# An order for every engine from one list scheduler at build time, in a streaming-encoder block on one core

## The chip, the core and the metric

The kernel runs on one core of a Trainium2 chip, as one launch. The metric is device time in microseconds (us); what is shown is the median of three runs. Below, PE is TensorE's matmul pipe and PEld its weight load, DVE is VectorE, ACT is ScalarE, POOL is GpSimd, SP is SyncE, whose queue issues nearly all DMAs. L319 is line 319 of the program named.

## The reference

256 tokens of width 2048 (`x`) and 256 memory tokens (`mem`) pass through one layer, all in float32; D_FF is 5632.

```python
x = x + 0.5 * swiglu(rms_norm(x, ffn1_norm), ffn1_w_gate, ffn1_w_up, ffn1_w_down)
h = rms_norm(x, mix_norm);  proj = h @ w_in
u, q, k, v, g, a_lr = split(proj)       # 1024 | 512 | 512 | 1024 | 1024 | 16 columns
y_pool = pool_mixer(u, pool_w, pool_scale)              # trailing means over 2/4/8/16 tokens
y_gla  = gla_mixer(q, k, v, g, a_lr, w_a2, b_a, head_norm)   # chunks of 64, 4 heads
x = x + concat([y_pool, y_gla]) @ w_out
x = x + mem_cross_attention(rms_norm(x, xattn_norm), rms_norm(mem, mem_norm), w_q, w_kv, w_o)
x = x + 0.5 * swiglu(rms_norm(x, ffn2_norm), ffn2_w_gate, ffn2_w_up, ffn2_w_down)
out = rms_norm(x, final_norm)
# swiglu(h, g, u, d) = (silu(h @ g) * (h @ u)) @ d
```

## The kernel before, in words

**Units.** All weights are streamed once, in units of 1 MB: a `raw` tile of 128 x 2048 floats. For precision, each unit is split in two: ACT casts `raw` to `wh` (the high part, in the chip's reduced float32 form), DVE subtracts `wh` from `raw` to give `wl` (the low part). Activations are split likewise (`xs` and `ys`, each with a high and a low half). PE then forms three products (high by high, high by low, low by high) and adds them in PSUM; a usual unit is 24 matmuls of 128 x 512. So every unit is a chain: a DMA on SP's queue, a cast on ACT, a subtraction on DVE, 24 matmuls on PE. There are three buffers each of `raw`, `wh` and `wl`. In these names the first number is the unit's: `wh24` is the high part of unit 24.

**Blocks.** Units are gathered in blocks which accumulate in PSUM. PSUM holds four tiles `ps` of two banks; each block takes two of them (`pt`), or four, or one, and gives them back when its results are evicted. `block_t` is the usual one. `block_s`, used for the gate and up projections of the two FFNs, takes three of its eight units (`PAIRS`, 0, 2 and 4) as seven products of sums in the place of eight: DVE makes sums `T` of weights (`add_weights`), and such a unit has a second pair of casts (`xh`, `xl`). It holds all four PSUM tiles; after its last unit, `combine` and `join` fold the four with additions on DVE into a tile `sg` in SBUF. A block behind it needs the PSUM tiles that these read.

**What stands between blocks.** `st.op(f, n)` hangs a piece of other work n units further on: the turning of the hidden layer's result (`turn`: 8 transposes `ph` on PE, a cast and a subtraction into `ys`), the next norm (`fold`: 8 transposes `px`, 8 scaled casts into `xs` on ACT and 8 on DVE, two squares for the norm on ACT), the mixer's and the attention's vector work. Program order is that of `Stream.emit`: splits run two units ahead of the matmuls.

**Who sets the order.** In the two FFN sections (`ordered(True)` to `ordered(False)`) DVE and ACT keep program order; there ACT and DVE run what `Stream.emit` wrote, whatever waits. Elsewhere, and on PE everywhere, the framework's own scheduler may reorder. At the start `x_squares` is held behind the scaled cast of its chunk by `tc.issue_after`. At the end `ready_sqrt` puts an activation with a square root on ACT, in program order, so that the function table is loaded before the last norm needs it.

**Places the prediction speaks of.** Unit 24 (the first unit of a `block_s` that stands behind another `block_s`, whose last two accumulators `pt44` and `pt45` its joins add into `sg46`); the fold around unit 129 between FFN1 and the mixer; the pool part's `k` additions around unit 151; the first four units; the last norm.

Of the kernel before, what the change touches and what calls it, by code (L numbers as in the profile page):

```python
# [1 line left out]

# [90 lines left out]
class Ordered:  # L93


    def __init__(self, tc, engine):
        self.tc, self.engine = tc, engine

    def __getattr__(self, name):
        f = getattr(self.engine, name)  # L100

        def call(*args, **kw):
            return self.tc.keep_in_program_order(f(*args, **kw))  # L103

        return call


class Engines:


    def __init__(self, tc):
        self.nc, self.ordered = tc.nc, False
        self.pinned = {n: Ordered(tc, getattr(tc.nc, n)) for n in ("vector", "scalar")}

    def __getattr__(self, name):
        if name in ("vector", "scalar") and self.ordered:
            return self.pinned[name]
        return getattr(self.nc, name)


def build(ctx, tc, I, out):
    nc = Engines(tc)
# [8 lines left out]
    scope = {"stack": None}  # L131

    def open_scope(name):
        def f():
            scope["stack"] = ExitStack()
            scope["pool"] = scope["stack"].enter_context(
                tc.tile_pool(name=name, bufs=1, reuse_waits="tile")
            )
        return f

    def close_scope():
        scope["stack"].close()
        scope["stack"] = None

    def ptile(name):
        return psum.tile([P, 2, NB], F32, tag="ps", name=name)
# [10 lines left out]
    def ctile():  # L157
        return scope["pool"].tile([P, 2, S], F32, tag="c", name=uid("c"), bufs=2)

    def ttile():  # L160
        return scope["pool"].tile([P, 2, S], F32, tag="t", name=uid("t"), bufs=3)
# [3 lines left out]
    def whole_lines(pool, shape, dt, tag, name, bufs=1):  # L165
# [4 lines left out]
        t = pool.tile([shape[0], -(-n // LINE) * LINE], dt, tag=tag, name=name, bufs=bufs)[:, :n]  # L170
# [10 lines left out]
    ident = head.tile([P, P], F32, tag="ident", name="ident")  # L181
    make_identity(tc.nc, ident)
    ones = const.tile([P, P], F32, tag="ones", name="ones")
# [13 lines left out]
    X = [dram.tile([S, 2 * NB], F32, tag=f"X{b}", name=f"X{b}") for b in range(2)]  # L197
    xs = main.tile([P, KT, 2, S], F32R, tag="xs", name="xs")
    ys = main.tile([P, KT, 2, S], F32R, tag="ys", name="ys")
# [28 lines left out]
    def diagonal(col):  # L228
        d = scope["pool"].tile([P, P], F32, tag="diag", name=uid("diag"), bufs=4)
        nc.vector.tensor_scalar_mul(d, ident, col)  # L230
        return d
# [20 lines left out]
    def row_squares(src, c):  # L252

        for h in range(2):
            j = tmp.tile([P, S], F32, tag="j", name=uid("j"), bufs=2)
            nc.scalar.activation(j, src[h], AF.Square, accum_out=ss[:, h, c : c + 1])
# [10 lines left out]
    def spread_norm():  # L267
# [4 lines left out]
        R = rows["R"] = scope["pool"].tile([P, S], F32, tag="R", name=uid("R"))  # L272
# [80 lines left out]
    def part_sums(act, ext, i, g):  # L353

        t = scope["pool"].tile([P, 4 * NB], F32, tag="T", name=uid("T"))
# [15 lines left out]
    def add_weights(u, raw):  # L371
        t = scope["pool"].tile([P, 4 * NB], F32, tag="T", name=f"T{u}")
# [9 lines left out]
    def split_seven(u, raw, t):  # L382
        th, tl = (
            wpool.tile([P, 4 * NB], F32R, tag=n, name=f"{n}{u}", bufs=st.AHEAD + 1)
# [5 lines left out]
        if True:  # L390
            r = [
                scope["pool"].tile([P, 3 * NB], F32R, tag=n, name=f"{n}{u}", bufs=2)
# [28 lines left out]
    def block_s(srcs, act, ext, pairs, evict, delays=(0, 0)):  # L421
# [32 lines left out]
        def combine():  # L454

            e = held["e"] = scope["pool"].tile([P, 4, NB], F32, tag="sg", name=uid("sg"), bufs=2)
# [89 lines left out]
    def gain_columns(names, queue):  # L546
        t = rows["gain"] = scope["pool"].tile([P, P], F32, tag="gain", name=uid("gain"), bufs=2)
# [11 lines left out]
    def x_tile(b):  # L559
        xrows[b] = scope["pool"].tile([P, 2, 2 * NB], F32, tag="sg", name=uid("x"), bufs=2)  # L560
# [35 lines left out]
    def x_squares(c):  # L596
        with tc.issue_after(rows["hi", c].ins):
            row_squares([x_cols(c * S, S)[:, h] for h in range(2)], c)
# [31 lines left out]
    def fold(c, gain):  # L630
# [10 lines left out]
        for h in range(2):  # L641
            q = tmp.tile([P, NB], F32, tag="j", name=uid("j"), bufs=2)
# [19 lines left out]
    def pair_sums(g, delay):  # L662
        def f():
            if g == PAIRS[0]:
                rows["xe"] = scope["pool"].tile(
# [11 lines left out]
    def ordered(on):  # L677
        def f():
            nc.ordered = on
        return f  # L680

    def ffn(wg, wu, wd, down):
        gate = {}
        st.op(ordered(True), 8)

        def hidden():
            e = scope["pool"].tile([P, 4, NB], F32, tag="sg", name=uid("sg"), bufs=2)
# [67 lines left out]
    st.op(ordered(False))  # L755
# [7 lines left out]
    def mt(name, shape, tag=None, bufs=1):  # L763
        t = whole_lines(scope["pool"], shape, F32, tag or name, uid(name), bufs)
# [14 lines left out]
    def m4():  # L779
        return scope["pool"].tile([P, 2 * 2 * (S + PAD)], F32, tag="m4", name=uid("m4"), bufs=3)  # L780
# [264 lines left out]
    def xt(name, shape, dt=F32, tag=None, bufs=1):  # L1045
        t = whole_lines(scope["pool"], shape, dt, tag or name, uid(name), bufs)
# [118 lines left out]
    def last_gain():  # L1165
        fin["gB"] = scope["pool"].tile([P, D], F32, tag="T", name="gB")
        nc.sync.dma_start(fin["gB"], I["final_norm"].partition_broadcast(P))

    def down_last(wd, k0, nk, last):
        if last:  # L1170
            st.op(ordered(False), 2)
# [4 lines left out]
    def down_end(wd, k0, nk):  # L1176
# [28 lines left out]
        def end_evict(nb, h):  # L1205
            cols = slice(nb * NB, (nb + 1) * NB)
            if h == 0:
                t = scope["pool"].tile([P, 3 * NB], F32, tag=("xh", "xl")[nb % 2], name=uid("O"), bufs=2)
# [38 lines left out]
        def ready_sqrt():  # L1247
            tc.keep_in_program_order(nc.scalar.activation(sums, Rcol, AF.Sqrt))
# [24 lines left out]
    def load(u):  # L1273
        raws[u] = wpool.tile([P, 4 * NB], F32, tag="raw", name=f"raw{u}", bufs=st.RAW)
        st.units[u][0](raws[u])

    def split_unit(u, own):
        raw = raws.pop(u)
        if own is split_seven:
            return split_seven(u, raw, summed.pop(u))  # L1280
        parts = [
            wpool.tile([P, 4 * NB], F32R, tag=t, name=f"{t}{u}", bufs=st.AHEAD + 1)
# [50 lines left out]
```

## Time and profile before

| what | value |
|---|---|
| time, three runs | 2141.07, 2144.1, 2147.86 us; median 2144.1 |
| profiled execution, first to last instruction | 2142.1 us |
| time of the profiled execution outside its span | not recorded; its span is 2.0 below the median of the runs |
| mean granted TensorE clock | 0.997 |
| PE busy | 2117.4 us, 99% of the span |
| DVE busy | 1434.5 us, 67% |
| ACT busy | 1004.6 us, 47% |
| bytes read from HBM | 417.58 MB, 203 GB/s over the span |

The profile is of one execution. A timeline row reads: start in us, length in us, engine, line, operation, result <- operands, sizes, count, and in brackets the idle time ahead of it with what released it. A row of the view of waits reads: engine, what waited, its line, <- what released it: total us, count, the longest. A windows row reads, for a stretch of time: its length, then for each engine its busy us and count, and then the granted PE clock, DMA share and GB/s. Busy time of PE is no measure of how well it is fed; its waits are.

### The profile page before, as it was taken

What the parts mean: (1) busy time and instruction counts of PE and PEld (TensorE: products, weight loads), DVE (VectorE), ACT (ScalarE), POOL (GpSimd) and SP (SyncE); (2) the same over time, 40 slices, a digit from 0 to 9 for tenths busy, and PEclk for the clock granted to TensorE, in tenths of its full rate; (3) what the DMA queues carried; (4) which work ended last, traced back from release to release, by engine and by line L of the source; (5) the groups of instructions that cost most, each with busy time, mean ns of one, the idle gap of its engine ahead of it and who ended that gap; (6) DMA issues with size and microseconds to landing.
All of it is one profiled execution on the core that took longest, in us unless ns stands there. A gap on an engine that the chain in (4) does not pass through costs nothing.

```text
span 2142.1 us, 24059 instructions
## 1 busy us (share of the span) xinstructions
PE 2117.4 (99%) x10032; PEld 1770.8 (83%) x10032; DVE 1434.5 (67%) x1189; ACT 1004.6 (47%) x890; POOL 14.2 (1%) x41
## 2 busy tenths in 40 slices
PE   9999999999999999999999999999999999999998
PEld 7878888888888888888888888888888888888886
DVE  8876588865874676565656545567974788658754
ACT  7544345533543545455445444445453454434533
POOL 0000000000000000000000000000000000000001
PEclk9999999999999999999999999999999999999999
DMA  7556565666566655558655455665666655766673
GB/s 276 177 176 240 212 216 180 209 240 214 197 216 236 218 163 175 177 154 300 228 184 177 157 160 174 197 206 188 198 233 220 212 200 184 252 211 212 216 236 118
DMA packets 143316, 435.91 MB, mean 203 GB/s; under 512 B 9828, under 2 KB 13000, under 8 KB 142824
## 3 DMA queue, kind: packets, MB, share of 16 engines
q1 hardware_dynamic: 143176, 434.38, 60.2%
q8 instruction: 78, 1.28, 0.2%
q14 instruction: 30, 0.25, 0.0%
q10 hardware_dynamic: 32, 0.01, 0.0%
HBM read 417.58 MB, written 16.78 MB: 203 GB/s over the span
## 4 chain that ended last, share of the span: by engine, by line
PE 96%; DVE 2%; ACT 1%; issue 1%; DMA 0%; SPq 0%; DVEq 0%; ACTq 0%
PE pt L319 57%; PE pa L304 15%; PE pt L416 11%; PE pb L319 6%; PE pe L319 3%; PE ph L712 1%; ACT wh L103 1%; PE pl L1106 1%; PE pv L1141 1%; PE px L636 0%; DVE T L103 0%; DVE wl L103 0%; DVE xl L103 0%; DMA x<-in_x 0%; ACT wh L246 0%
## 5 line engine op out<-in xcount | busy, mean ns | idle before, releaser
L319 PE MATMUL pt<-wh,xs 128*128 128x512 f32 x1952 | 618.6, 391 | 0.0
L103 DVE TENSOR_TENSOR wl<-raw,wh 128x2048 fp32r<-128x2048 f32 x186 | 425.1, 2289 | 246.4 <-ACT wh L103 246.4
L319 PE MATMUL pt<-wh,ys 128*128 128x512 f32 x1728 | 535.2, 390 | 0.0
L103 ACT CAST wh<-raw 128x2048 fp32r<-128x2048 f32 x186 | 355.1, 1914 | 378.9 <-PE pt L319 326.5
L247 DVE TENSOR_TENSOR wl<-raw,wh 128x2048 fp32r<-128x2048 f32 (+2 forms) x142 | 314.6, 2216 | 254.5 <-ACT wh L246 254.2
L319 PEld LDWEIGHTS pt<-wh,xs 128*128 128x128 f32 x1952 | 368.0, 189 | 76.3
L246 ACT CAST wh<-raw 128x2048 fp32r<-128x2048 f32 (+2 forms) x143 | 263.1, 1840 | 281.9 <-PE pt L319 96.1
L319 PE MATMUL pt<-wl,xs 128*128 128x512 f32 x976 | 381.3, 391 | 0.0
L319 PEld LDWEIGHTS pt<-wh,ys 128*128 128x128 f32 x1728 | 324.4, 188 | 67.1
L319 PE MATMUL pt<-wl,ys 128*128 128x512 f32 x864 | 336.4, 389 | 1.4 <-DVE wl L103 1.4
L304 PE MATMUL pa<-xs,wh 128*128 128x512 f32 x896 | 317.2, 398 | 2.1 <-DVE t L278 1.7
L304 PE MATMUL pa<-xs,wl 128*128 128x256 f32 x896 | 248.7, 281 | 0.0
L319 PEld LDWEIGHTS pt<-wl,xs 128*128 128x128 f32 x976 | 184.2, 189 | 37.9
L304 PEld LDWEIGHTS pa<-xs,wh 128*128 128x128 f32 x896 | 167.7, 188 | 41.4 <-issue 2.0
L319 PEld LDWEIGHTS pt<-wl,ys 128*128 128x128 f32 x864 | 162.2, 188 | 35.1 <-DVE wl L103 1.9
L103 ACT CAST wh<-T 128x2048 fp32r<-128x2048 f32 x52 | 99.4, 1912 | 151.5 <-PE pt L319 93.2
L304 PEld LDWEIGHTS pa<-xs,wl 128*128 128x128 f32 x896 | 169.1, 189 | 1.6 <-issue 0.2
L103 DVE TENSOR_TENSOR wl<-T,wh 128x2048 fp32r<-128x2048 f32 x52 | 119.0, 2289 | 55.6 <-ACT wh L103 55.2
L319 PE MATMUL pb<-wh,xs 128*128 128x512 f32 x384 | 121.7, 392 | 0.5 <-DVE ys L239 0.5
L416 PE MATMUL pt<-wh,xe 128*128 128x512 f32 x324 | 112.4, 391 | 0.2
L103 DVE TENSOR_TENSOR sg<-pt,sg 128x1024 f32<-128x1024 f32 (+1 forms) x90 | 90.1, 1008 | 6.4 <-ACT sg L103 5.1
L103 DVE TENSOR_TENSOR xl<-raw,xh 128x1536 fp32r<-128x1536 f32 x52 | 91.1, 1751 | 0.0
(213 smaller groups left out, 1820.3 us busy)
## 6 DMA issues: line engine op xcount, KB each, us to landing
raw<-in_ffn_w_down SPq DMA_DIRECT2D x88, 1024.0 KB, 5.4
raw<-in_ffn_w_up SPq DMA_DIRECT2D x80, 1024.0 KB, 5.0
raw<-in_ffn_w_gate SPq DMA_DIRECT2D x77, 1024.0 KB, 5.0
raw<-in_w_in SPq DMA_DIRECT2D x32, 1024.0 KB, 5.2
raw<-in_xattn_w_kv SPq DMA_DIRECT2D x32, 1024.0 KB, 5.2
raw<-in_w_out SPq DMA_DIRECT2D x16, 1024.0 KB, 6.2
raw<-in_xattn_w_q SPq DMA_DIRECT2D x16, 1024.0 KB, 5.2
raw<-in_xattn_w_o SPq DMA_DIRECT2D x16, 1024.0 KB, 5.6
```

The lines of the kernel that those rows point to most:

```text
L103: return self.tc.keep_in_program_order(f(*args, **kw))
L246: nc.scalar.copy(hi, src)
L247: nc.vector.tensor_tensor(out=lo, in0=src, in1=f32(hi), op=ALU.subtract)
L304: nc.tensor.matmul(o, w, x, start=k == 0 and i == 0, stop=last and i == 1)
L319: nc.tensor.matmul(ps, a, w, start=first and i == 0, stop=last and i == 2)
L416: nc.tensor.matmul(banks[n], x, w, start=first and j == 0, stop=not later and n in ("P1", "P5", "P6", "P7") and j == 2,)
L712: nc.tensor.transpose(v[:, i, h * P : (h + 1) * P], g[:, h, i * P : (i + 1) * P], ident)
L1106: nc.tensor.matmul(ps[:, t, :M], ys[:, 4 * h + d, a, tok], xa["K"][:, d, b, :], start=i == 0, stop=i == 11,)
L1141: nc.tensor.matmul(ps[:, d, :S], xa["V"][:, m, a, col], xa["PT"][:, m, b, :], start=i == 0, stop=i == 5,)
```

## The change

Calls such as `nc.vector.tensor_tensor(...)` no longer issue an instruction. A `Recorder` writes each down as a `Task` with the tiles that it reads and writes, and of each tile the cells (64 elements wide, and the rows of partitions) that it touches; two tasks depend on each other if they touch a common cell and one writes. Buffers of a pool are dealt out by `share`: the next user of a place depends on all users of the one before. Each task has a modelled duration (`cost`). `latest` works back from the end along PE's program order to the latest start that holds nothing up; `schedule` then plays the engines forward: PE takes the ready task that is first in program order, the others take, among those ready within `WAIT` (0.2 us), the one with the earliest deadline, with a shorter one ahead if it fits the gap. `emit` issues all in order of the planned starts, and each is kept in that order. `Ordered`, `Engines`, `ordered` and `issue_after` are gone; `ready_sqrt` is recorded as any other task. What is computed, with which instructions on PE, stays as it was.

```diff
-class Ordered:
-    def __init__(self, tc, engine):
-        self.tc, self.engine = tc, engine
+def cost(engine, name, args, kw, writes, reads):
...
+    if name == "dma_start":
+        v = (writes or reads)[0]
+        return dict(busy=0.37, moved=(v.p1 - v.p0) * v.at.size * 4)
+    if engine == "tensor":
+        n = writes[0].at.size
+        busy = 0.2284 if n > 256 else 0.118 if n > 128 else 0.109
+        if name == "matmul" and args[1].dtype is F32:
+            busy = 0.1 + n / 600
+        return dict(busy=busy, tail=0.177)
+    if engine == "scalar":
+        out = writes[0].at.size
+        busy = (0.05 if psum else 0.085) + out * 0.84e-3
...
+        table = {AF.Silu: "silu", AF.Sqrt: "sqrt", AF.Exp: "exp", AF.Ln: "exp"}.get(func)
+        return dict(busy=busy, tail=0.1, table=table)
+    if engine == "vector":
...
+        return dict(busy=(0.13 if name == "scalar_tensor_tensor" else 0.07) + n / 960, tail=0.085)
...
+class Plan:
+    SYNC = 0.034
...
+    def share(self):
+        for bufs, line in self.places.values():
+            held = [None] * bufs
+            for b in sorted((b for b in line if b.users), key=lambda b: b.users[0].i):
+                k = min(range(bufs), key=lambda k: held[k].users[-1].i if held[k] else -1)
+                old, held[k] = held[k], b
+                if old is None:
+                    continue
+                gate = self.add(None, None)
+                for u in old.users:
+                    self.dep(gate, u, False)
+                for u in b.users:
+                    self.dep(u, gate, True)
...
+    def touch(self, t, v, write):
+        b = v.buf
...
+        for c in v.cells():
+            spans = b.cells.setdefault(c, [])
+            keep = []
+            for s in spans:
+                p0, p1, wrote, u = s
+                if p0 < v.p1 and v.p0 < p1:
+                    if write or wrote:
+                        self.dep(t, u, wrote)
+                    if write and v.p0 <= p0 and p1 <= v.p1:
+                        continue
+                keep.append(s)
+            keep.append((v.p0, v.p1, write, t))
+            b.cells[c] = keep
...
+    def ready(self, t, end):
+        r = 0.0
+        for p, data in t.preds.items():
+            if p.engine is None:
+                x = p.start
+            elif p.engine == t.engine and not p.moved and (p.engine == "tensor" or not data):
+                x = p.start + p.busy
+            else:
+                x = end[p.i] + self.SYNC
+            r = max(r, x)
+        return r
+
+    def latest(self):
...
+                left[s.i] -= 1
+                if not left[s.i]:
...
+            late = -t.busy - t.tail
+            for s in t.succs:
+                if t.engine is None:
+                    x = s.late
+                elif t.moved:
+                    x = s.late - 1.8 - t.moved / 338e3
+                elif s.engine == t.engine and (t.engine == "tensor" or not s.preds[t]):
+                    x = s.late - t.busy
+                else:
+                    x = s.late - t.busy - t.tail - self.SYNC
+                late = min(late, x)
+            if t in behind:
+                late = min(late, behind[t].late - t.busy)
+            t.late = late
+
+    def schedule(self):
+        self.share()
+        self.latest()
...
+        def pick(e):
+            q, now = waiting[e], free[e]
+            if e == "tensor":
+                now = max(now, min(t.start for t in q))
+                t = min((t for t in q if t.start <= now), key=lambda t: t.i)
+                return now, t
+            soon = max(now, min(t.start for t in q))
+            u = min((t for t in q if t.start <= soon + self.WAIT), key=lambda t: t.late)
+            if u.start > soon:
+                fit = [t for t in q if t.start <= soon and soon + t.busy <= u.start]
+                if fit:
+                    u = min(fit, key=lambda t: t.late)
+            return max(now, u.start), u
...
+                tables[e] = t.table
+                busy += 1.28
+            free[e] = at + busy
+            end[t.i] = at + busy + t.tail
+            if t.moved:
...
+        self.end = end
+        out = [t for _, _, t in sorted((t.start, k, t) for k, t in enumerate(out))]
+        return out
+
+    WAIT = 0.2
+
+    def emit(self):
+        for t in self.schedule():
+            if t.engine is None:
+                if t.run:
+                    t.run()
+            else:
+                self.tc.keep_in_program_order(t.run())
+
+class Recorder:
...
+            plan, e = self.plan, self.engine
...
+            def run():
+                real = lambda a: a.resolve() if isinstance(a, View) else a
+                f = getattr(getattr(plan.tc.nc, e), name)
+                return f(*(real(a) for a in args), **{k: real(a) for k, a in kw.items()})
+            t = plan.add(e, run, **cost(e, name, args, kw, writes, reads))
...
+            for v in reads:
+                plan.touch(t, v, False)
+            for v in writes:
+                plan.touch(t, v, True)
...
-class Engines:
...
 def build(ctx, tc, I, out):
-    nc = Engines(tc)
+    nc = plan = Plan(tc)
...
     def x_squares(c):
-        with tc.issue_after(rows["hi", c].ins):
-            row_squares([x_cols(c * S, S)[:, h] for h in range(2)], c)
+        row_squares([x_cols(c * S, S)[:, h] for h in range(2)], c)
...
     def ffn(wg, wu, wd, down):
         gate = {}
-        st.op(ordered(True), 8)
...
         def ready_sqrt():
-            tc.keep_in_program_order(nc.scalar.activation(sums, Rcol, AF.Sqrt))
+            nc.scalar.activation(sums, Rcol, AF.Sqrt)
...
     st.emit(load, prepare, split_unit)
+    plan.emit()
```

The order on the engines changes in many places; these are the ones on which the prediction rests. In the changed kernel every operation has the line of the recorder, L469.

**PE around unit 23** (`ph48` and `ph49` are the two transposes of FFN1's first hidden tiles, which read `sg36`; `pt44`, `pt45` the last two accumulators of the block then running). Before, inside unit 23, `ph48` standing in the same way in unit 22:

```order
L319 MATMUL pt44_847<-wh23_1001,xs_107 128x512
L319 MATMUL pt45_848<-wh23_1001,xs_107 128x512
L319 MATMUL pt44_847<-wl23_1002,xs_107 128x512
L712 MATMUL ph49_1045<-ident_73,sg36_560 128x128 x8
L319 MATMUL pt44_847<-wh23_1001,xs_107 128x512 x2
L319 MATMUL pt44_847<-wl23_1002,xs_107 128x512
```

Now:

```order
L469 MATMUL pt45_855<-wh21_930,xs_138 128x512
L469 MATMUL pgain47_1026<-ident_73,gain35_91 128x128
L469 MATMUL ph48_1028<-ident_73,sg36_538 128x128 x8
L469 MATMUL ph49_1041<-ident_73,sg36_538 128x128 x8
L469 MATMUL pt44_847<-wh22_962,xs_138 128x512
L469 MATMUL pt44_847<-wl22_975,xs_138 128x512
```

Both groups of transposes and `pgain47` now stand ahead of unit 22.

**DVE around units 24 to 26** (`T26` is the sum of weights for unit 26; `sg46` takes the results in `pt44` and `pt45` and so gives their PSUM back). Before:

```order
L103 TENSOR_TENSOR ys_108<-ph48_1034,ys_108 128x4x256
L103 TENSOR_TENSOR ys_108<-ph49_1045,ys_108 128x4x256
L103 TENSOR_TENSOR wl24_1057<-T24_997,wh24_1056 128x2048
L103 TENSOR_TENSOR xl24_1061<-raw24_939,xh24_1060 128x1536
L103 TENSOR_TENSOR T26_1090<-raw26_1005 128x1024
L103 TENSOR_TENSOR T26_1090<-T26_1090,raw26_1005 128x512 x2
L103 TENSOR_TENSOR wl25_1095<-raw25_969,wh25_1094 128x2048
L103 TENSOR_TENSOR sg46_992<-pt44_847,sg46_992 128x1024
L103 TENSOR_TENSOR sg46_992<-pt45_848,sg46_992 128x1024
```

Now:

```order
L469 TENSOR_TENSOR xl24_1048<-raw24_955,xh24_985 128x1536
L469 TENSOR_TENSOR ys_1044<-ph48_1028,ys_1044 128x4x256
L469 TENSOR_TENSOR wl24_1071<-T24_1007,wh24_1056 128x2048
L469 TENSOR_TENSOR ys_1044<-ph49_1041,ys_1044 128x4x256
L469 TENSOR_TENSOR T26_1090<-raw26_1030 128x1024
L469 TENSOR_TENSOR T26_1090<-T26_1090,raw26_1030 128x512
L469 TENSOR_TENSOR wl25_1104<-raw25_990,wh25_1092 128x2048
L469 TENSOR_TENSOR sg46_972<-pt44_847,sg46_972 128x1024
L469 TENSOR_TENSOR T26_1090<-T26_1090,raw26_1030 128x512
L469 TENSOR_TENSOR sg46_972<-pt45_855,sg46_972 128x1024
```

`ys48`, the copy of the first transposes, has moved behind `xl24`, and `wl24` between it and `ys49`; the addition from `pt44` stands before the last part of `T26`, and that from `pt45` behind it.

**ACT at the start** (`px` are the transposes of `x`, `j` the squares for the first norm, `chain` the square root; `wh3` the cast of the fourth unit). Before:

```order
L246 CAST wh2_212<-raw2_132 128x1024
L238 ACTIVATE xs_107<-px11_283,gains_97 128x256
L256 ACTIVATE j27_460,ss_100<-x3_125 128x256
L256 ACTIVATE j28_462,ss_100<-x3_125 128x256
L238 ACTIVATE xs_107<-px12_322,gains_97 128x256
L246 CAST xe14_376<-T16_385 128x512
L246 CAST wh3_253<-raw3_167 128x2048
```

Now:

```order
L469 ACTIVATE xs_138<-px10_277,gains_122 128x256 x2
L469 ACTIVATE j31_295,ss_129<-x3_147 128x256
L469 ACTIVATE j32_299,ss_129<-x3_147 128x256
L469 ACTIVATE j33_302,ss_129<-x3_147 128x256
L469 ACTIVATE j34_306,ss_129<-x3_147 128x256
L469 CAST xe14_231<-T16_257 128x512
L469 ACT_TABLE_LOAD
L469 ACTIVATE chain_314<-chain_314 128x2
L469 CAST wh3_332<-raw3_194 128x2048
```

The squares, the load of the square root's table and the square root stand ahead of `wh3`.

**ACT at the fold around unit 129** (`px114`, `px117` the transposes of the new `x`). Before:

```order
L103 CAST wh128_4547<-raw128_4457 128x2048
L103 ACTIVATE xs_107<-px114_4579,gains_97 128x256 x4
L103 ACTIVATE j115_4596,ss_100<-x111_4420 128x512
L103 ACTIVATE j116_4598,ss_100<-x111_4420 128x512
L103 ACTIVATE xs_107<-px117_4600,gains_97 128x256 x4
L103 ACTIVATE j118_4617,ss_100<-x111_4420 128x512
L103 ACTIVATE j119_4619,ss_100<-x111_4420 128x512
L103 CAST wh129_4621<-raw129_4487 128x2048
```

Now:

```order
L469 CAST wh128_4549<-raw128_4479 128x2048
L469 ACTIVATE j115_4561,ss_129<-x111_4128 128x512
L469 ACTIVATE j116_4566,ss_129<-x111_4128 128x512
L469 ACTIVATE j118_4569,ss_129<-x111_4128 128x512
L469 ACTIVATE j119_4572,ss_129<-x111_4128 128x512
L469 CAST wh129_4592<-raw129_4509 128x2048
L469 ACTIVATE xs_138<-px114_4589,gains_122 128x256 x4
L469 ACTIVATE xs_138<-px117_4600,gains_122 128x256 x4
```

The cast of unit 129 has moved ahead of the eight scaled casts into `xs`.

295 lines of the change are left out of this document (243 added, 52 removed).

## The prediction

> **What bounds the kernel now.** I read the page first: the span, the busy times and the chain that ended last.
>
> ```profile
> span 2142.1 us, 24059 instructions
> PE 2117.4 (99%) x10032; PEld 1770.8 (83%) x10032; DVE 1434.5 (67%) x1189; ACT 1004.6 (47%) x890; POOL 14.2 (1%) x41
> PE 96%; DVE 2%; ACT 1%; issue 1%; DMA 0%; SPq 0%; DVEq 0%; ACTq 0%
> ```
>
> PE carries the chain almost from end to end, and the change leaves it the same matmuls. So no more can be won than PE's pauses and the slow stretches that they cause; everything else is under it. The second view is the list of PE's waits:
>
> ```profile
> PE pt L416 <- DVE sg L103: 4.5, 1, 4.5
> PE pgain L554 <- DMA gain<-in_ffn_norm: 4.1, 1, 4.1
> PE pa L304 <- DVE t L278: 1.7, 1, 1.7
> PE pt L319 <- DVE wl L103: 1.4, 1, 1.4
> PE po L976 <- DVE ST L969: 1.0, 1, 1.0
> PE pp L827 <- DVE k L278: 0.6, 1, 0.6
> PE pb L319 <- DVE ys L239: 0.5, 1, 0.5
> PE pa L304 <- DVE xs L239: 0.4, 1, 0.4
> ```
>
> One large wait, six that DVE ends, and the first load (4.1), which no order shortens. Without that load they are 10.1 us. The third view is the windows around the large one, with PE's busy time, its count and, third from the right, its granted clock:
>
> ```profile
> 143.00:148.00 5.00, 0.57 (x3) 0.14 (x1) 4.93 (x6) 0.00 (x0) 0.00 (x0) 0.92 0.65 213
> 148.00:154.00 6.00, 5.93 (x14) 4.67 (x15) 2.66 (x3) 5.89 (x7) 0.00 (x0) 0.50 0.52 173
> 154.00:160.00 6.00, 6.00 (x27) 4.95 (x27) 5.93 (x6) 2.50 (x2) 0.00 (x0) 1.00 0.39 127
> ```
>
> After the pause PE does 14 matmuls in 6 us at clock 0.50, where it does 27 in the next 6 us. At 6.0/27 = 0.222 us each, 14 are worth 3.1, so the slow stretch lost 2.9 us. The pause costs 4.5 + 2.9 = 7.4 us in all. All that is recoverable is then 10.1 + 2.9 = 13.0 us, 0.6% of the span.
>
> **The change part by part.** *The pause at 143 us.*
>
> ```profile
> 128.78 1.03 PE L712 MATMUL ph<-ident,sg 128*128 128x128 f32 x8
> 135.28 1.01 ACT L103 CAST ys<-ph 128x1024 fp32r<-128x1024 f32 x1 [4.42 <-PE ph L712]
> 136.33 1.23 DVE L103 TENSOR_TENSOR ys<-ph,ys 128x1024 fp32r<-128x1024 f32 x1 [4.21 <-ACT ys L103]
> 138.13 2.29 DVE L103 TENSOR_TENSOR wl<-T,wh 128x2048 fp32r<-128x2048 f32 x1 [0.58 <-ACT wh L103]
> 139.89 0.39 PE L416 MATMUL pt<-xh,xs 128*128 128x512 f32 x1
> 140.34 1.75 DVE L103 TENSOR_TENSOR xl<-raw,xh 128x1536 fp32r<-128x1536 f32 x1
> 142.01 1.22 DVE L103 TENSOR_TENSOR T<-raw 128x1024 f32<-128x1024 f32 x1
> 146.80 2.35 DVE L103 TENSOR_TENSOR sg<-pt,sg 128x1024 f32<-128x1024 f32 x2
> 148.07 0.79 PE L416 MATMUL pt<-xh,xs 128*128 128x512 f32 x1 [4.50 <-DVE sg L103]
> ```
>
> The cause is order. ACT and DVE keep program order, and the second transpose's copy (135.28) stands before the cast of unit 24, so both engines idle more than 4 us for a transpose inside unit 23. Then the subtractions `wl24` (2.29), `xl24` (1.75), the sums `T` and `wl25` are all ahead of the two additions that give PSUM back (146.80), and PE waits. In the new order both transposes come before unit 22, at about 127.1 to 129 (16 transposes, twice the 1.03 less overlap), so their casts are done by 132: one cast (1.01), the cast of `wh24`, the second cast. DVE then has, from 129.2 on, `xl24` 1.75, a copy 1.23, `wl24` 2.29, a copy 1.23, a part of `T` 1.22 and about 0.7 for a half of the next, `wl25` about 2.3: 10.7 us, to 139.9. The addition from `pt44` can start when unit 23 ends, at 139.9 + 0.39 = 140.3, and ends at 141.5; the next, behind 0.7 of `T`, at 143.4. PE wants `pt44` at about 143.2, where the old stall began, and `pt45` three matmuls later, 143.9. So the wait goes, with some 0.5 us to spare for the second, and the slow stretch with it: **-7.4**. What is late next would be these additions again, if `T` or `wl25` came 1 us later than I count.
>
> *The fold.*
>
> ```profile
> 704.48 0.47 ACT L103 ACTIVATE xs<-px,gains 128x256 fp32r<-128x256 f32 x1 [4.41 <-PE px L636]
> 713.82 1.90 ACT L103 CAST wh<-raw 128x2048 fp32r<-128x2048 f32 x1
> 718.10 0.50 PE L319 MATMUL pt<-wl,ys 128*128 128x512 f32 x1 [1.44 <-DVE wl L103]
> ```
>
> ACT spends 704.48 to 713.82 on eight scaled casts and four squares before it casts unit 129. The casts now come behind it; at 0.47 each that is at least 3.8 us earlier, more than the wait: **-1.4**. The casts are wanted only by the mixer's first units, behind the rest of FFN1.
>
> *The mixer.*
>
> ```profile
> 832.87 0.69 DVE L278 TENSOR_TENSOR k<-pa,c 128x512 f32<-128x512 f32 x1 [1.41 <-ACT c L277]
> 834.89 2.29 DVE L247 TENSOR_TENSOR wl<-raw,wh 128x2048 fp32r<-128x2048 f32 x1 [0.53 <-ACT wh L246]
> 837.10 0.68 DVE L278 TENSOR_TENSOR k<-pa,c 128x512 f32<-128x512 f32 x1
> ```
>
> A `wl` of 2.29 us stands between two additions of which PE wants the second; now both additions stand before it (wait 0.6, and 0.5 behind it). The others in the list are alike (0.4, 1.0 with its two steps no longer back to back, 1.7 where an accumulator is asked for a unit later). Together 4.2; I leave 0.8 standing, since the 1.7 hangs on an addition behind another long subtraction: **-3.4**. Bounds: 0 to 4.2.
>
> *The start, a loss.*
>
> ```profile
> 11.93 0.47 ACT L238 ACTIVATE xs<-px,gains 128x256 fp32r<-128x256 f32 x1 [0.91 <-PE px L590]
> 22.41 1.91 ACT L246 CAST wh<-raw 128x2048 fp32r<-128x2048 f32 x1
> 24.41 2.28 DVE L247 TENSOR_TENSOR wl<-raw,wh 128x2048 fp32r<-128x2048 f32 x1
> 24.58 0.41 ACT L256 ACTIVATE j<-x 128x256 f32<-128x256 f32 x1
> 26.80 0.60 PE L590 MATMUL px<-ident,x 128*128 128x128 f32 x4
> 42.07 1.28 ACT L217 ACT_TABLE_LOAD   x1
> ```
>
> The cast of unit 3 is at 22.41. Ahead of it ACT now has six more squares (6 x 0.41 = 2.5), three scaled casts fewer (3 x 0.47 = 1.4), and the table load of 1.28 that stood at 42.07, with its square root of 0.2: +2.6. It starts at 25.0 and the subtraction ends 4.3 later (22.41 to 24.41 + 2.28 = 26.69 before), at 29.3. PE now gets to unit 3 at about 26.5, since the four transposes at 26.80 and two like them are placed elsewhere. It can fill 1.1 us with the second half of one chunk's transposes and the first high-by-high products: a pause of about 1.7. Lower bound 0, since ACT idles here now (0.91 in the row at 11.93); upper bound 2.8 without the filling, and with a slow stretch of 2.9 as at 148 it would be 5.7. I take **+1.0**, nearer the low end because ACT's idle time takes part of the work.
>
> The Trainium skill, "TensorE: Matmul & The Clock Gate", Part 1 on the HAM clock gate, says that PE falls to half clock after an idle window of about 3.4 us. By that rule a pause of 2.8 here would leave the clock alone and the upper bound would be 2.8; the one pause of this trace that bears on it (4.5 us, then 0.50) agrees but does not show where the limit lies.
>
> *The hand-overs between blocks.* Nine `block_s` in each FFN end in two joins. The planner takes the ready operation with the earliest deadline, so a `T` or `wl` of the next unit may now stand ahead of a join, or between two.
>
> ```profile
> L103 DVE TENSOR_TENSOR sg<-pt,sg 128x1024 f32<-128x1024 f32 (+1 forms) x90 | 90.1, 1008 | 6.4 <-ACT sg L103 5.1
> ACT xs L238 <- DVE xs L239: 24.3, 21, 2.4
> ```
>
> A join or combine step is an addition of about 1.0 us, and PE wants the next block's accumulators as soon as the last unit ends. The second row shows what the model does not hold: ACT waits for DVE between two reads of one PSUM tile (24.3 us in 21 waits), while the planner, which goes by cells, takes reads of different cells as independent. So planned times can be short. Lower bound 0; upper bound 18 x 0.6 (the wait behind `k` above) = 11. Nearest are the single waits of 0.4 to 0.6, and in most blocks DVE has room: **+1.0**.
>
> The Trainium skill, "PSUM — Partial Sum Buffer", section on bank collisions, asks that two engines not be in one PSUM bank at once, and that software guard it by bank. By that rule the planner's cells are too fine and its order too hopeful; the sum would then go to the upper bound of this term, a rival below.
>
> *The tail.*
>
> ```profile
> 2128.37 0.19 ACT L1214 ACTIVATION_READ_ACCUMULATOR O<-x 128x1 f32 x1
> 2129.82 0.19 ACT L217 ACTIVATE chain<-chain 128x1 f32<-128x1 f32 x1
> ```
>
> The early square root is recorded without a place and is issued so long before that a table load comes back at the end. Between these rows 2129.82 - 2128.56 = 1.26 us are free, and the load takes 1.28: **0**. Without that cover it costs 1.3.
>
> Sum: -7.4 - 1.4 - 3.4 + 1.0 + 1.0 = -10.2 (-12.2 and +2.0). The profiled execution's span becomes 2131.9. It lies 2.0 below the median of the three runs shown (2144.1), so the time is 2144.1 - 10.2 = **2133.9**, called 2134.
>
> **The rivals.** *Most of it is given back* (2138 to 2147). One way: the start takes its 5.7, and the 18 blocks 0.2 each (3.6): 12.2 - 9.3 = 2.9 gained, 2141. The other: the additions from `pt44` stay late and the first term does not come; 4.8 - 2.0 = 2.8, 2141 again. For it: the margin of 0.5 us at 143, and the cells against tiles. Against: both engines idled over 4 us there, which the new order uses.
>
> *Slower than before.* The mechanism is the same collision at other block joins: transposes, casts and `wl` before the additions, in a stretch where DVE has no slack.
>
> ```profile
> 350.00:400.00 50.00, 50.00 (x230) 41.36 (x229) 46.47 (x37) 25.15 (x16) 0.00 (x0) 1.00 0.56 191
> ```
>
> DVE is busy 46.5 of 50 us here, and PE none the less without a pause (50.00): a late addition has 3.5 us in which to catch up. A join that is late as at 143 costs 7.4. Two of them (14.8) eat the 10.2 and leave +4.6, inside what counts as no change; three (22.2) leave +12, 2156. It decides from the second. Against: in the new order an addition stands directly behind the subtraction that it used to follow at a distance.
>
> *More is gained* (2126 to 2129): the losses do not come and the 0.8 that I left in the mixer goes too, all of the 13.0, 2131.1; and the median falls by as much as the fastest run shown lies below the others' median (2144.1 - 2141.07 = 3.0), 2128. Nothing in the order speaks for more: PE's pace stays.
>
> **How the numbers follow.** What can be told from no change here is about 0.3%, 6.4 us, so faster means below 2137.7 and slower above 2150.5. Forecast case 0.62 (2129 to 2138); more gained 0.10; given back 0.20; slower 0.08. Faster: 0.62 + 0.10 less a little at the edge, 0.71; slower 0.08; no change 0.21. For the range, I cut half of the case of more (0.05 left below 2127) and, above 2145, the slower case and a little of the given-back one (0.10): 2127 to 2145.
>
> **What would show it.** Right: no PE wait for `sg` near 143 us, and clock 1.00 from 143 to 160; the wait for `wl` near 716 gone; the cast of unit 3 at about 25 us, with a PE pause of 1 to 2 us behind it at full clock; the list of PE's waits without the load at 1 to 4 us. Wrong: waits of `pt` for `sg` or `ys` in several blocks; windows at clock 0.50 other than the first 10 us; a start pause beyond 3 us; the last square root later behind the squares than 1.3 us. A PE busy time that moves with an equal count of matmuls would mean that the pace itself has changed, which I count at nothing.

## The result, and the profile after

The changed kernel takes 2155.86 us (median of 4 runs, 2155.2 to 2156.81) where the kernel before takes 2142.97 (median of 4, the three runs of the table above and one more): a ratio of 1.0056, 95% interval 1.0042 to 1.0070. It is slower by 12.9 us between the medians, clear of the noise. 2134 was predicted, with a range from 2127 to 2145.

The page of the changed kernel:

```profile
span 2154.9 us, 24105 instructions
PE 2120.2 (98%) x10032; PEld 1770.8 (82%) x10032; DVE 1431.3 (66%) x1189; ACT 1000.1 (46%) x888; POOL 15.8 (1%) x41
PE 96%; ACT 2%; DMA 1%; DVE 1%; issue 0%; SPq 0%; DVEq 0%; ACTq 0%
```

The matmuls are as many. PE's busy time is 2.8 us more; a matmul that has waited counts longer in the profile (0.50 us in the row at 57.12 below, where the prediction's row at 139.89 has 0.39). In the chain, ACT has gone from 1% to 2% and DVE from 2% to 1%. PE's waits, without those for the first loads:

```profile
PE pt L469 <- ACT sg L469: 8.3, 6, 2.7
PE pq L469 <- DVE ST L469: 4.0, 8, 0.6
...
PE pt L469 <- DVE sg L469: 1.8, 2, 0.9
PE pb L469 <- ACT v L469: 1.6, 2, 0.8
...
PE pp L469 <- ACT ys L469: 1.1, 2, 0.6
PE pt L469 <- DVE wl L469: 0.8, 1, 0.8
PE ps L469 <- DVE m L469: 0.8, 1, 0.8
PE pt L469 <- ACT wh L469: 0.7, 1, 0.7
PE px L469 <- ACT xs L469: 0.6, 1, 0.6
PE tm L469 <- ACT xs L469: 0.6, 1, 0.6
```

Not one of the waits of the kernel before is left: the 4.5 for `sg` at 143 us, the 1.7, 1.4, 1.0, 0.6, 0.5 and 0.4 are gone. In their place stand ten kinds, 20.3 us in 25 waits (before 10.1 in the 7 that the prediction counts). The pause at 143 went as predicted; the window of the changed kernel there, PE busy and its clock third from the right:

```profile
143.00:148.00 5.00, 5.00 (x23) 4.14 (x23) 4.94 (x5) 1.45 (x3) 0.00 (x0) 1.00 0.27 48
```

The two longest of the new waits, 2.47 and 2.74 us, are where the first block of each FFN ends. This block and the last one with a gate half are the FFN's two gate blocks in what follows: both are `block_t`, whose results ACT (silu) or DVE takes straight from PSUM, and the waits in their last units are the gate hand-overs. Rows of PE and ACT from the changed kernel's timeline, at the first of them:

```profile
53.17 1.90 ACT L469 CAST wh<-raw 128x2048 fp32r<-128x2048 f32 x1
54.04 0.61 PE L469 MATMUL pt<-wh,xs 128*128 128x512 f32 x2
55.08 1.28 ACT L469 ACT_TABLE_LOAD   x1
56.38 0.69 ACT L469 ACTIVATE sg<-pt,Rcol 128x512 f32<-128x512 f32 x1
57.12 0.50 PE L469 MATMUL pt<-wl,xs 128*128 128x512 f32 x1 [2.47 <-ACT sg L469]
57.88 0.69 ACT L469 ACTIVATE sg<-pt,Rcol 128x512 f32<-128x512 f32 x1 [0.82 <-PE pt L469]
```

Read them from PE's side. A block ends with three matmuls into each half (bank) of an accumulator `pt`: `wh`, `wl`, `wh`. At 54.04 PE has done the last of the first half and the first of the second. The next one, `wl` into the *second* half, waits until ACT has read the *first* half (the silu at 56.38). ACT is at a cast, then loads a table, then reads. The data do not ask for that: the two halves have nothing in common but the tile. The same shape stands in the mixer, PE and DVE:

```profile
866.13 0.65 PE L469 MATMUL pq<-m,k 128*64 128x256 f32 x4
866.83 0.42 DVE L469 COPY ST<-pq 64x256 f32<-64x256 f32 x1 [1.84 <-PE pq L469]
867.30 0.43 PE L469 MATMUL pq<-m,k 128*64 128x128 f32 x2 [0.53 <-DVE ST L469]
```

and the wait for `ST` is DVE's reading of a part of `pq` in one bank while PE has a part in the other bank to write.

To see where the time went, I took from the timelines the time between the starts of neighbouring matmuls, and from it the usual pace (0.227 us for 512 columns, 0.117 for 256, 0.109 for 128). What is left over, summed by stretch (us; how the few smaller matmuls are priced moves 800 to 1000 and the total by up to 2 us, in all columns alike):

| stretch | before | after | psum_by_tile | tile_squares_later |
|---|---|---|---|---|
| 0 to 100 (start; first gate block at 54) | 4.0 | 10.6 | 7.9 | 4.7 |
| 100 to 200 (the pause at 143) | 8.7 | 0.2 | 0.8 | 0.5 |
| 600 to 700 (a gate block) | 0.3 | 2.4 | 0.2 | 0.3 |
| 700 to 800 (fold, mixer) | 3.9 | 2.2 | 1.5 | 1.4 |
| 800 to 1000 (mixer) | 9.9 | 17.9 | 5.6 | 5.6 |
| 1400 to 1500 (first gate block of FFN2) | 0.1 | 5.7 | 0.1 | 0.1 |
| 2000 to 2100 (a gate block) | 0.3 | 2.4 | 0.2 | 0.2 |
| all | 30.8 | 43.8 | 17.9 | 14.3 |

The last two columns are experiments below. After less before is +13.0, the spans' difference 12.8. In the column of the changed kernel the eight waits at the four gate blocks make 14.1, one slow stretch (half clock, at 1472 us) included; a second one, at 902, is in the mixer's 17.9.

### The profile page after: what moved, and what is told of

It is laid out like the page before. It is cut to its first block, busy times and chain, and to the rows that moved or that the text cites. A ratio compares the mean times of both kernels' runs of the same rounds, so it can differ in the third digit from the quotient of the medians.

```text
span 2154.9 us, 24105 instructions
## 1 busy us (share of the span) xinstructions
PE 2120.2 (98%) x10032; PEld 1770.8 (82%) x10032; DVE 1431.3 (66%) x1189; ACT 1000.1 (46%) x888; POOL 15.8 (1%) x41
## 4 chain that ended last, share of the span: by engine, by line
PE 96%; ACT 2%; DMA 1%; DVE 1%; issue 0%; SPq 0%; DVEq 0%; ACTq 0%
PE pt L469 68%; PE pa L469 15%; PE pb L469 6%; PE pe L469 3%; PE ph L469 1%; ACT wh L469 1%; PE px L469 1%; PE pv L469 1%; PE pl L469 1%; DMA raw<-in_ffn_w_up 1%; DMA raw<-in_ffn_w_gate 0%; DVE wl L469 0%; DMA x<-in_x 0%; PE po L469 0%; PE pq L469 0%
## 5 line engine op out<-in xcount | busy, mean ns | idle before, releaser
L469 DVE TENSOR_TENSOR wl<-raw,wh 128x2048 fp32r<-128x2048 f32 (+2 forms) x328 | 740.8, 2259 | 570.2 <-ACT wh L469 569.0
L469 ACT CAST wh<-raw 128x2048 fp32r<-128x2048 f32 (+2 forms) x329 | 618.5, 1880 | 788.4 <-PE pt L469 559.8
L469 PE MATMUL pt<-wh,xs 128*128 128x512 f32 x2060 | 649.1, 391 | 0.7 <-ACT wh L469 0.7
L469 PE MATMUL pt<-wh,ys 128*128 128x512 f32 x1728 | 535.4, 390 | 0.0
L469 PEld LDWEIGHTS pt<-wh,xs 128*128 128x128 f32 x2060 | 388.4, 189 | 81.3 <-ACT wh L469 0.9
L469 PE MATMUL pt<-wl,xs 128*128 128x512 f32 x1030 | 403.0, 391 | 10.9 <-ACT sg L469 8.3
L469 PEld LDWEIGHTS pt<-wh,ys 128*128 128x128 f32 x1728 | 324.4, 188 | 67.0
L469 PE MATMUL pt<-wl,ys 128*128 128x512 f32 x864 | 336.2, 389 | 0.0
L469 PE MATMUL pa<-xs,wh 128*128 128x512 f32 x912 | 321.2, 398 | 0.0
L469 PE MATMUL pa<-xs,wl 128*128 128x256 f32 x896 | 249.0, 281 | 0.0
L469 PEld LDWEIGHTS pt<-wl,xs 128*128 128x128 f32 x1030 | 194.1, 188 | 54.4 <-ACT sg L469 10.9
L469 PEld LDWEIGHTS pa<-xs,wh 128*128 128x128 f32 x912 | 171.4, 188 | 39.7 <-issue 0.3
L469 PEld LDWEIGHTS pt<-wl,ys 128*128 128x128 f32 x864 | 162.2, 188 | 33.5
L469 PEld LDWEIGHTS pa<-xs,wl 128*128 128x128 f32 x896 | 169.8, 190 | 1.2
L469 ACT CAST wh<-T 128x2048 fp32r<-128x2048 f32 x54 | 103.4, 1915 | 129.2 <-PE pt L469 77.9
L469 DVE TENSOR_TENSOR wl<-T,wh 128x2048 fp32r<-128x2048 f32 x54 | 123.6, 2288 | 24.2 <-ACT wh L469 24.1
L469 PE MATMUL pb<-wh,xs 128*128 128x512 f32 x384 | 121.8, 392 | 0.0
L469 ACT CAST xh<-raw 128x1536 fp32r<-128x1536 f32 x54 | 80.0, 1482 | 77.5 <-DMA raw<-in_ffn_w_gate 39.3
L469 PE MATMUL pt<-wh,xe 128*128 128x512 f32 x324 | 108.5, 389 | 0.0
L469 DVE TENSOR_TENSOR xl<-raw,xh 128x1536 fp32r<-128x1536 f32 x54 | 94.6, 1751 | 0.0
L469 DVE TENSOR_TENSOR sg<-pt,sg 128x1024 f32<-128x1024 f32 (+1 forms) x90 | 89.9, 1006 | 1.1
L469 PEld LDWEIGHTS pb<-wh,xs 128*128 128x128 f32 x384 | 72.1, 188 | 14.8
```

The source lines that it names most:

```text
L469: return f(*(real(a) for a in args), **{k: real(a) for k, a in kw.items()})
```

## The experiments

**Two theories.** T: the planner takes reads and writes of different cells of one PSUM tile as independent, and issues an eviction between two matmuls into the same tile; but the program makes a matmul wait for any earlier-issued read of its tile, whatever part. O: the order by deadlines itself brings evictions late, behind casts and a table load; told of the guard, the planner would only move the waits.

**psum_by_tile**, the planner told of the guard:

```diff
-        self.grain = 1 if n <= 128 else 64
+        self.grain = n if psum else 1 if n <= 128 else 64
```

> One line: in the planner every PSUM buffer is one cell, so that any write into a PSUM tile depends on every read of that tile. Theory T (tile guard): the changed kernel plans reads and writes of different parts of one PSUM tile as independent, while the program makes PE wait for a read of any part of the tile. Then the gate hand-overs (14.1 us from start to start at 54, 59, 658, 662, 1468, 1475, 2073 and 2077 us), the mixer's waits (10.5) and the two at px and tm (1.5) go: 2155.9 - 26.1 = 2130, 2126 to 2135. The start stays late. Rival O (order): the order by deadlines itself brings the evictions late, behind casts and a table load on ACT; told of the guard the planner only moves the waits, at most a third of them goes: 2147 or more.

2130.51 us (2129.81 to 2131.79), ratio to before 0.9949 (0.9932 to 0.9965). T, to half a microsecond. (The kernel before, run alongside in each sitting, had medians from 2141.8 to 2143.0, so differences between runs of different sittings are good to about 1 us.) The whole list of PE's waits in this run:

```profile
PE px L469 <- DMA x<-in_x: 4.5, 2, 3.9
PE pt L469 <- DVE wl L469: 1.6, 1, 1.6
PE pt L469 <- ACT wh L469: 0.9, 1, 0.9
PE ph L469 <- DVE gains L469: 0.5, 1, 0.5
```

and at the first gate block ACT still comes after a cast and a table load:

```profile
55.58 1.28 ACT L469 ACT_TABLE_LOAD   x1
56.88 1.27 ACT L469 ACTIVATE sg<-pt,Rcol 128x512 f32<-128x512 f32 x2
```

The silu is no earlier than in the changed kernel (56.88 against 56.38), and PE does not notice.

**psum_by_tile_pt** and **psum_by_tile_rest**, the same for a part of the tiles, in `Plan.tile` (shown for the tiles `pt`; for the rest the condition on the name is turned round):

```diff
         b = Buf(shape, None, scope, psum=pool is not None and pool is self.psum, dtype=dt)
+        if b.psum and name.startswith("pt"):
+            b.grain = 1024
```

> The same for the block accumulators named pt alone (FFN, output projections), cells as before for all other PSUM tiles. T: the 14.1 us of the gate hand-overs go, the mixer's stay: 2155.9 - 14.1 = 2142, 2139 to 2145; PE's list keeps pq <- ST (4.0) and pb <- v (1.6) and loses sg. O: 2150 or more.

2143.46 us (2141.84 to 2144.33), ratio 1.0006 (0.9997 to 1.0016): 12.4 less than the changed kernel, against 14.1 expected. PE's list has lost `sg`; the mixer's are as they were:

```profile
PE pq L471 <- DVE ST L471: 4.0, 8, 0.6
...
PE pb L471 <- ACT v L471: 1.6, 2, 0.8
```

> The same for all PSUM tiles but pt. T: the mixer's 10.5 and the 1.5 at px and tm go, the gate hand-overs stay: 2155.9 - 12.0 = 2144, 2140 to 2147; PE's list keeps sg (8.3 and 1.8) and loses pq, pb, px, tm. If the mixer's waits are for the data and not for the tile (theory D: a product needs what DVE has just written), they stay: 2154.

2141.42 us (2140.11 to 2143.51), ratio 0.9998 (0.9989 to 1.0008): 14.4 less than the changed kernel, against 12.0 expected. The mixer's waits are gone, so they were not for the data (theory D falls), and `sg` is back:

```profile
PE pt L471 <- ACT sg L471: 7.4, 6, 2.5
...
PE pt L471 <- DVE sg L471: 1.8, 2, 0.9
```

12.4 + 14.4 = 26.8, against 25.4 for both at once: the two parts nearly add up.

**psum_by_bank**, two cells for the two banks of a tile:

```diff
-        self.grain = 1 if n <= 128 else 64
+        self.grain = NB if psum else 1 if n <= 128 else 64
```

> As psum_by_tile, but a PSUM buffer of two banks is two cells, one for each bank, so that the planner guards by bank. If the program guards by bank (theory B), it is as psum_by_tile: 2130.5. If it guards the whole tile (theory T in its narrow form), the planner still puts a read of the first bank between matmuls into the second: the eight gate hand-overs stay (14.1), the two pb <- v too, and only waits between parts of one bank go (px 0.7, tm 0.7, a part of the eight at pq): 2155.9 - 3 to 6 = 2151, 2148 to 2154.

2156.52 us (2155.99 to 2157.05), ratio 1.0065 (1.0048 to 1.0081): nothing is won. The gate hand-overs stay, as the narrow form of T says, and so do all eight at `pq`:

```profile
PE pt L469 <- ACT sg L469: 7.5, 6, 2.5
...
PE pq L469 <- DVE ST L469: 4.0, 8, 0.6
```

So the program's guard is the whole tile of two banks, and a planner that knows banks alone is no better off here than one that knows cells. That a part of `pq` would go, and the waits at `px` and `tm`, was a miss: all are as they were (4.0, 0.6 and 0.6). For `pq` the kernel shows why: the matmul that waits at 867.30 above writes the second bank, while DVE reads the first.

**before_gains_later**, the prediction's first term alone, in the kernel before:

```diff
-    st.op(lambda: turn_gains(G_MIX, G_END), 22)
+    st.op(lambda: turn_gains(G_MIX, G_END), 24)
```

> The kernel before with one number changed: the transposes of the gains come two units later (24 for 22), so that both hidden transposes stand ahead of unit 22 as in the changed kernel; DVE and ACT keep program order. By the prediction's first term the pause at 143 us goes and nothing else changes: 2143.0 - 7.4 to 8.7 = 2135, 2133 to 2138. Rival: the pause only moves to the next join, because DVE still does T and wl before the additions: 2140 to 2144.

2134.22 us (2133.12 to 2136.08), ratio 0.9965 (0.9953 to 0.9976): one number in the kernel before is worth 7.9 us. DVE's copies from the transposes now stand together, the additions come 6 us earlier, and the window is full (DVE rows, then the window):

```profile
128.90 2.36 DVE L103 TENSOR_TENSOR ys<-ph,ys 128x1024 fp32r<-128x1024 f32 x2
...
140.44 2.34 DVE L103 TENSOR_TENSOR sg<-pt,sg 128x1024 f32<-128x1024 f32 x2
```

```profile
143.00:148.00 5.00, 5.00 (x24) 4.14 (x23) 1.86 (x1) 5.00 (x6) 0.00 (x0) 1.00 0.35 140
```

The pause did not move to another join.

**The start.** In the changed kernel (ACT, then PE):

```profile
24.57 1.28 ACT L469 ACT_TABLE_LOAD   x1
...
25.98 1.88 ACT L469 CAST wh<-raw 128x2048 fp32r<-128x2048 f32 x1
```

```profile
27.91 1.20 PE L469 MATMUL pt<-wh,xs 128*128 128x512 f32 x4 [0.68 <-ACT wh L469]
...
30.24 0.49 PE L469 MATMUL pt<-wl,xs 128*128 128x512 f32 x1 [0.79 <-DVE wl L469]
```

**tile_squares_later** is psum_by_tile with the 16 squares made dependent on the cast of unit 3; **tile_squares_gains_later** holds back the small gain transfers too:

```diff
     def x_squares(c):
-        row_squares([x_cols(c * S, S)[:, h] for h in range(2)], c)
+        row_squares([x_cols(c * S, S)[:, h] for h in range(2)], c, rows["cast", 3])
...
-            nc.scalar.activation(j, src[h], AF.Square, accum_out=ss[:, h, c : c + 1])
+            t = nc.scalar.activation(j, src[h], AF.Square, accum_out=ss[:, h, c : c + 1])
+            plan.dep(t, behind, True)
```

> psum_by_tile, and the 16 squares of the first norm wait for the cast of unit 3. What is left of PE's waits in psum_by_tile stands at 26 to 30 us: 1.07 + 1.76 + 0.29 = 3.1 us from start to start. If the squares, the table load and the square root ahead of that cast are the cause (the prediction's step on the start, taken there at 1.0), 2130.5 - 3.1 = 2127.4, 2126 to 2129. If unit 3 waits for its transfer instead (its DMA stands behind the gains on SP's queue), less than 1 us goes: 2130.

2127.47 us (2126.67 to 2127.66), ratio 0.9930 (0.9913 to 0.9947).

> The same, and the seven small gain transfers on SP's queue wait for the cast of unit 3 as well. If the squares alone are the cause, as tile_squares_later (2127.4); if the transfer of unit 3 is, this one goes to 2127 and tile_squares_later stays at 2130.

2127.32 us (2126.81 to 2128.97), ratio 0.9930 (0.9915 to 0.9945). The squares, with the table load and the root behind them, were the cause, 3.0 us; the transfer was not. About half of it is a slow stretch that stands behind the two waits in psum_by_tile (clock 0.50 from 29.5 to 32.9 us) and comes in neither of these two runs. tile_squares_later beats both kernels, by 14 us the kernel before and by 28 the changed one. Its waits, without the first loads:

```profile
PE pt L469 <- DVE wl L469: 0.7, 1, 0.7
PE ph L469 <- DVE gains L469: 0.2, 1, 0.2
```

**after_silu_early**, the changed kernel with the silu table loaded ahead of time (its cells as they were):

```diff
         rsqrt(Rcol, sums, D, 2)
+        if not spread_too:
+            early = tile_of(tmp, [P, S], F32, tag="j", name=uid("j"), bufs=2)
+            nc.scalar.activation(early[:, :2], Rcol, AF.Silu)
```

> The changed kernel with one activation of 2 columns with the silu function behind each norm that an FFN follows, so that the table stands ready before the gate's evictions. It measures the part of the table load in the long waits at 54 and 1468 us. By T the wait is for a read of the tile that is planned between its matmuls, whatever else ACT does: only the two loads (2 x 1.28) and the slow stretch behind the longer wait (1.8) go: 2155.9 - 4.4 = 2151.5, 2149 to 2154; six sg waits stay. If late evictions on ACT were the cause (theory O), the two hand-overs would be clean: 2155.9 - 2.7 - 1.0 - 4.8 - 1.0 = 2146.

2151.33 us (2150.1 to 2152.2), ratio to before 1.0041 (1.0026 to 1.0056): 4.5 less than the changed kernel, where 4.4 were expected. Part of this agreement is chance: the slow stretch at 902 us has gone too, which the expectation did not count, and one at 30 us has come. The waits are all there, each now of at most 0.8 us, where a silu takes 0.69:

```profile
PE pt L469 <- ACT sg L469: 4.7, 6, 0.8
...
PE pt L469 <- DVE sg L469: 1.8, 2, 0.9
```

O had 2146. The table load made two of the waits long; it is not why they are there.

**tile_reads_too**, reads of one tile by two engines made dependent as well, in `touch`:

```diff
-                    if write or wrote:
+                    if write or wrote or b.psum and u.engine != t.engine:
```

> psum_by_tile, and reads of one PSUM tile by two engines depend on each other in the planner too, as the program makes ACT wait for DVE between casts of one tile. If only PE's waits matter: no change, 2130.5, within 1.5. If the plan's times for ACT and DVE at folds and evictions are too hopeful without it: faster by 1 to 3.

2137.98 us (2136.14 to 2140.14), ratio 0.9979 (0.9970 to 0.9989): 7.5 *slower* than psum_by_tile. Neither expectation had that. About 5 us of it stand between 1100 and 1200 us (counted as in the table, 5.8 here and 0.7 in psum_by_tile), around the first wait below and a slow stretch behind it; the rest was not separated. The largest of PE's waits in this run, then ACT's row for the casts of a fold, then the same row in psum_by_tile:

```profile
PE pa L469 <- DVE xs L469: 3.5, 1, 3.5
```

```profile
ACT xs L469 <- DVE xs L469: 23.6, 27, 2.4
```

```profile
ACT xs L469 <- DVE xs L469: 0.2, 1, 0.2
```

ACT's waits between casts of one tile, 24.3 in the kernel before, had gone to 0.6 in the changed kernel and 0.2 in psum_by_tile without anybody asking for it, and came back to 23.6 when the planner was told of them. It put each cast behind DVE's read of the part before; left alone, it issues all casts ahead of DVE's reads. So the wait between two readers follows the order in which they are issued. It costs where an order alternates them, and a planner that believes in it makes it true.

## Why the prediction was wrong

**The step that failed is the term on the hand-overs between blocks**, "+1.0". Its mechanism was in front of me and I drew the wrong consequence. I quoted ACT waiting for DVE on one PSUM tile, said that the planner's cells do not hold that, and then counted readers against readers and joins that DVE does too late. What costs is PE's *write* against a *read* of the same tile that has been issued ahead of it; it needs no late engine. It costs 25.4 us in all (the step from the changed kernel to psum_by_tile), 12.4 of it at the gate blocks (psum_by_tile_pt) and the rest mainly in the mixer, where the sum had no term of this kind; I had +1.0, and 18 blocks at 0.6 as the upper bound, 11 us. I had also looked in the wrong place: the 18 blocks that I counted are `block_s`, and the gate blocks are `block_t`. No wait of the list is for a join; the places are eight at the gates, eight at `pq`, and seven others, most of them in the mixer. It could have been seen in the order of issue: a read by ACT whose start is planned when the first half of a tile is complete must stand, in the order of issue, ahead of the matmuls into the other half.

The page on PSUM of the Trainium skill ("PSUM — Partial Sum Buffer", section "PSUM bank collisions raise a hardware error"), which the prediction set beside this term, asks for a guard by bank; the runs show the program's guard to be by tile (psum_by_bank, 2156.5, is no better than the changed kernel), and two readers of one tile to cost PE nothing where they are issued in one go (psum_by_tile).

**The pause at 143 us**, -7.4: right. before_gains_later has it alone, -7.9; in the table it is -8.5. The spare half microsecond at the addition from `pt45` was enough.

**The fold and the mixer's old waits**, -1.4 and -3.4: right as far as they go, since every one of those waits is gone from the list; but the same stretches received new ones. From 700 to 1000 us the table has 13.8 before and 20.1 after; only in psum_by_tile, with 7.1, does the gain show, 6.7 where 4.8 were predicted.

**The start**, +1.0: the mechanism was right, the size too small. The cast of unit 3 is at 25.98 (25.0 said), PE's two waits are 0.68 and 0.79 (1.7 said in one). Counted as in the table, 20 to 50 us has 0.3 before and 2.4 in the changed kernel, at full clock; in psum_by_tile, with its slow stretch, it has 4.8, and there holding the squares back wins 3.0. I had let ACT's idle time take part of the work; ACT has none between 16 and 26 us.

**The tail**, 0: right; from the last matmul's start to the end 10.0 us before and 9.8 after.

**The rivals.** "Slower than before" came out, and its 2156 is the time measured, but not by its mechanism, so that the agreement is luck: no join is late, and the waits are not of 7.4 us each but of 0.5 to 2.7. Of what I wrote down as showing me wrong, the profile shows waits of `pt` for `sg` in several blocks and two stretches at clock 0.50, at 902 and 1472 us. With the guard told, my sum for the rest (-12.2 + 1.0) stands close: 2130.5 measured where it gives 2131.8 from the 2143.0 of the kernel before. This is in part luck as well: by the table the start cost 2.9 more than I counted, while the pause, the fold and the mixer gave 2.4 more and stretches without a term 2.2.

## What to carry to other kernels

A planner that fixes the order of issue has to use the same unit of dependence as the layer that sets the semaphores: finer cells are not just a hopeful estimate of time, they issue reads between writes and so create waits that nothing in the data asks for. When a schedule replaces a program order, look in the new order for an eviction that stands between two writes into one tile, and price that. And when a kernel has one large pause, move the one operation first: here one number in the kernel before won 7.9 of the 14 us that the scheduler won once it knew the tiles and held the squares back.

## What the runs showed of the hardware that I had not expected

Windows, PE's granted clock third from the right. The changed kernel, after the two long waits, of 2.47 and of 2.74 us:

```profile
54.00:57.00 3.00, 0.65 (x3) 0.19 (x2) 2.97 (x3) 2.97 (x3) 0.00 (x0) 1.00 0.65 264
57.00:60.00 3.00, 2.88 (x12) 2.18 (x12) 2.96 (x4) 0.75 (x2) 0.00 (x0) 1.00 0.43 86
```

```profile
1468.00:1471.00 3.00, 0.30 (x2) 0.00 (x0) 3.00 (x3) 2.96 (x3) 0.00 (x0) 1.00 0.04 18
1471.00:1475.00 4.00, 3.96 (x11) 3.14 (x12) 1.33 (x1) 0.69 (x1) 0.00 (x0) 0.60 0.97 324
```

The first cost no clock, the second, hardly longer, brought it to 0.60 for 4 us. And after the two short waits at the start, 31 to 35 us, in the changed kernel and in after_silu_early:

```profile
31.00:35.00 4.00, 4.00 (x19) 3.27 (x18) 4.00 (x4) 1.92 (x2) 0.00 (x0) 1.00 0.88 281
```

```profile
31.00:35.00 4.00, 4.00 (x13) 3.14 (x12) 3.66 (x4) 3.08 (x3) 0.00 (x0) 0.67 0.77 257
```

In these two PE had waited for the same two things, 0.7 and 0.8 us each; one kept its clock and one fell to 0.67. So a slow stretch does not need a pause of 3.4 us, the figure that the prediction cited from the Trainium skill ("TensorE: Matmul & The Clock Gate", Part 1), and the length of a pause alone does not tell whether one follows.

The traces show what else counts. In every run the clock is 1.00 or 0.50 from about 11 us to the last few us, a slow stretch lasts one or two steps of 3.41 us, and it begins a whole number of such steps after the clock record begins (in the changed kernel at 10.9 us; 901.8 and 1471.8 are 261 and 428 steps later). Cut at these steps, the changed kernel's two long waits, then the short ones of the changed kernel and of after_silu_early, read:

```profile
55.29:58.70 3.41, 1.58 (x7) 1.32 (x8) 3.38 (x4) 2.45 (x3) 0.00 (x0) 1.00 0.20 80
1468.41:1471.82 3.41, 0.78 (x3) 0.67 (x4) 3.41 (x3) 2.57 (x4) 0.00 (x0) 1.00 0.26 30
```

```profile
27.98:31.39 3.41, 2.62 (x11) 1.78 (x12) 3.41 (x4) 3.41 (x6) 0.00 (x0) 1.00 0.07 20
```

```profile
26.84:30.26 3.42, 1.98 (x9) 1.20 (x9) 2.71 (x3) 3.39 (x7) 0.00 (x0) 1.00 0.07 25
```

The wait of 2.47 us lies across a step's edge, that of 2.74 in one step, of which PE was idle for 2.6; the two short waits lie in two steps in the changed kernel and in one, idle for 1.4, in after_silu_early. Over the profiles of all the runs, between the first 11 and the last 15 us, each of the six steps in which PE was idle for 1.9 us or more was followed by a slow one, and no slow stretch followed a step idle for less than 1.4. In between both occur (1.83 us in the step from 55.29 kept the clock, 1.4 lost it), so that idle time in the step is not all that decides.
